# The value products of the decoded streams: probabilities as the stationary operand on four column strips, and one transpose behind

## The chip, the cores and the metric

The kernel runs on one core of a Trainium2 chip. A time is the device time in microseconds (us) of one execution of the whole program; of several executions the median is given. The matrix engine is called PE in the rows, its loading of the stationary operand PEld, VectorE DVE, ScalarE ACT, GpSimd POOL, and the engine that issues most transfers SP.

## What is computed

One step of a hybrid encoder layer: an input projection, three token mixers (banded softmax attention, gated DeltaNet, a diagonal state space model), an output projection and a feed-forward network, for 2048 new prompt frames and for 8 running streams of 16 frames each, all in float32. The change is in the attention of the running streams:

```python
def band_attention_sample(q, k, v, k_cache, v_cache, table):
    kk = jnp.concatenate([k_cache, k], axis=1)      # 512 cached + 16 new rows, 8 heads x 64
    vv = jnp.concatenate([v_cache, v], axis=1)
    s = einsum('bqhd,bkhd->bhqk', q, kk) * d_h ** -0.5 + rel_bias(table, rel)
    p = softmax(s, axis=-1)
    return einsum('bhqk,bkhd->bqhd', p, vv)         # the line that the change is about
```

## The kernel before

The program has three stages in time: the projections together with DeltaNet and the state space model (to about 915 us), the attention (to about 1250 us), and the output projection with the feed-forward network. `attention` goes over 16 tiles of 128 prompt frames (`i`), and in each over 4 pairs of heads (`p`). A round is one pair: scores into PSUM tiles of the pool `asp` (4 buffers, called `aps` in the rows), minimum and exponential (`a_scores`), division by the sum (`a_norm`), transposes of the probabilities through PSUM tiles `tps` (pool `atp`, 3 buffers) into `PT` (`a_turn`), and the products with the values into `aob` (`a_values`). Rounds overlap: the values of a round are written two rounds after its scores.

In the tiles i = 1 to 8 one decoded stream (b = i - 1) is worked beside the prompt: `s_scores` and `s_norm` at p = 0, `s_turn` at p = 1, `s_values` at p = 2. The 8 heads are handled as 4 pairs. The probabilities of a stream stand in one tile `sP` of 128 rows (4 pairs x 2 heads x 16 frames) by 528 keys; `s_turn` transposes them into `sPT` (5 blocks of keys by 128 rows). `sV` holds the cached values (4 blocks of 128 keys by 512 columns, one head each 64 columns), `sVn` the new ones with zero rows below. `s_values` before: for each pair p, five products are summed; the values of the pair (128 keys by 128 columns) are the stationary operand, the 32 columns of the pair in `sPT` move over them, and the result stands with the value columns on the partitions, both heads crossed with both; two copies on VectorE keep the two matching quarters in `sos`, which goes to memory after the eighth stream.

`s_scores` already puts its four pairs on four strips of 32 columns of the array (`ps[p * 32:p * 32 + 32]`), and `a_values` puts its two heads on two strips of 64.

A scheduler sets each engine's order from the program's order and its own estimates, so the rows of an engine can move around an edit, but each engine works its own list in order. The line numbers are those of the kernel before; behind the edit those of the changed kernel are two to six higher.

Of the kernel before, what the change touches and what calls it, by code (L numbers as in the profile page):

```python
# [9 lines left out]
F32 = mybir.dt.float32  # L10
# [31 lines left out]
class K:  # L42
# [1027 lines left out]
    def attention(self, es):  # L1070
        nc, A = self.nc, self.A
        c = self.pool("ac", 1, es=es, side="right")
        self.ak = self.pool("ak", 2, es=es, side="right")
        self.asp = self.pool("asp", 4, PSUM, es=es, side="right")
        self.sc = self.pool("sc", 1, es=es)
        self.sw = self.pool("sw", 1, es=es)
        self.aw = self.pool("aw", 2, es=es)
        self.atp = self.pool("atp", 3, PSUM, es=es)
        self.aop = self.pool("aop", 1, PSUM, es=es)
        nb = self.nb = c.tile([128, 8, 640], F32, name="nb", tag="nb")  # L1080
        r = A["relrev"]
        for h in range(8):
            rv = self.aw.tile([128, 1024], F32, name="rv", tag="qd")[:, 0:640]
            nc.sync.dma_start(rv, bass.AP(tensor=r.tensor, offset=r.offset + h * 767, ap=[[1, 128], [1, 640]]))
            nc.scalar.activation(nb[:, h], rv[:, ::-1], AF.Copy, scale=-1.0)
        nc.gpsimd.memset(nb[0:64, :, 576:640], 1e30)
        nc.gpsimd.memset(nb[64:128, :, 0:64], 1e30)
        self.vt, self.ld_ = {}, {}

        self.kst = [c.tile([128, 8, 512], F32R, name=f"kst{i}") for i in range(2)]  # L1090
        for k in self.kst:
            nc.gpsimd.memset(k[:, :, 128:192].bitcast(F32), 0.0)

        self.qlz = [c.tile([128, 8, 128], F32R, name=f"qlz{i}") for i in range(2)]
        for z in self.qlz:
            for q in range(2):
                nc.gpsimd.memset(z[64 - q * 64:128 - q * 64, q::2].bitcast(F32), 0.0)
        self.sample_setup(es)
        for k in range(2):
            self.a_load_k(k)  # L1100
            self.a_keys(k)
        self.a_load_q(0)
        t = self.a_tile(0)
        for q in range(2):
            self.a_queries(t, q)


        rounds = []
        sample = None
        self.s_load_k(0)  # L1110
        self.s_load_v(0)
        for i in range(16):
            b = i - 1
            streams = 0 <= b < 8
            t1 = None
            for p in range(4):
                if p == 0:
                    if i < 14:
                        self.a_load_k(i + 2)
                    if i < 15:  # L1120
                        self.a_load_q(i + 1)
                elif p == 1 and i < 14:
                    self.a_keys(i + 2)
                elif p == 2 and i < 15:
                    t1 = self.a_tile(i + 1)
                    self.a_queries(t1, 0)
                elif p == 3 and i < 15:
                    self.a_queries(t1, 1)
                if streams and p == 0:
                    sample = self.s_scores(b)  # L1130
                    if b < 7:
                        self.s_load_k(b + 1)
                if streams and p == 2:
                    self.s_values(b, sample)
                    if b < 7:
                        self.s_load_v(b + 1)
                rounds.append(self.a_scores(t, p))
                self.a_norm(rounds[-1])
                if streams and p == 0:
                    self.s_norm(sample)  # L1140
                if len(rounds) > 2:
                    self.a_values(rounds.pop(0))
                if len(rounds) > 1:
                    self.a_turn(rounds[0])
                if streams and p == 1:
                    self.s_turn(sample)
                if p == 3 and i >= 8:
                    self.w_part(i - 8)
            t = t1
            if i == 8:  # L1150
                nc.sync.dma_start(self.mixT[0:512, SEQ:NT].rearrange("(f p) t -> p f t", p=128), self.sos)

        w0 = c.tile([128, 5, 8, 128], F32, name="w0", tag="nb")
        self.a_values(rounds.pop(0))
        self.a_turn(rounds[0])
        self.a_values(rounds.pop(0))
        self.y0 = self.wp.tile([128, 8, 128], F32, name="y0", tag="wor")
        h, l = (w0[:, i].bitcast(F32R) for i in (1, 2))
        self.w_in(0, w0[:, 0], self.y0, h, l)
        self.w_tile(0, self.y0, h, l, lambda: self.asp.tile([128, 512], F32, name="aps", tag="s"))  # L1160
# [177 lines left out]
        nc.gpsimd.memset(PT[:, 4], 0.0)  # L1338
        self.nc.vector.tensor_copy(PT[0:16, 4], ps[0:16, 0:128])

    def s_values(self, b, s):
        PT, vt = s["PT"], self.sV
        ob = self.asp.tile([128, 4, 128], F32, name="aps", tag="s")

        for p in range(4):
            out, hs, qs = ob[:, p, 0:32], slice(p * 128, p * 128 + 128), slice(p * 32, p * 32 + 32)
            for j in range(4):
                self.nc.tensor.matmul(out, vt[:, j, hs], PT[:, j, qs], start=j == 0, stop=False)
            self.nc.tensor.matmul(out, self.sVn[:, hs], PT[:, 4, qs], start=False, stop=True)
        bs = slice(b * 16, b * 16 + 16)  # L1350
        for q in range(2):
            rr = slice(q * 64, q * 64 + 64)
            self.nc.vector.tensor_copy(self.sos[rr, :, bs], ob[rr, :, q * 16:q * 16 + 16])


    def rsqrt1(self, pool, var, eps, tag, pin):
# [542 lines left out]
```

## Time and profile before

| | |
|---|---|
| median of 3 runs | 2916.17 us (2914.97 to 2923.32) |
| the profiled execution | 2905.62 us |
| its span, first to last instruction | 2903.8 us |
| busy: PE, DVE, ACT, POOL | 2787.1, 1946.7, 1314.6, 1096.8 us |
| mean granted clock of PE | 0.983 |

The profile gives, for one execution, when each instruction ran on its engine, what it waited for, and the clock that was granted to the matrix engine as a share of 2.4 GHz (0.50 is 1.2 GHz). A float32 product is recorded as two passes, so a count of PE in a view is twice the number of products in the code; a transpose is one pass. A view by stretches gives, for each stretch, its length, the busy time of each engine in it, the granted clock, and what the transfers did.

### The profile page before, as it was taken

The numbers are of one execution on the slowest core, as the hardware profiler recorded it, in microseconds if no ns is written. First come the engines' busy times: TensorE is split into PE (matmuls) and PEld (weight loads), VectorE is DVE, ScalarE is ACT, GpSimd is POOL, SyncE is SP. The second block draws the span as 40 slices with busy tenths as digits, with TensorE's granted clock in tenths as the row PEclk, the third lists the DMA queues.
The fourth block names the chain that finished last, engine by engine and source line by source line (L and its number), as shares of the span: only waits on it lengthen the run. The fifth ranks groups of instructions, "written<-read, shape, count | busy, mean of one in ns | idle before, by whom it ended". The sixth has DMA issues, their size and how long they took to land.

```text
span 2903.8 us, 46362 instructions
## 1 busy us (share of the span) xinstructions
PE 2787.1 (96%) x16677; PEld 2453.4 (84%) x16677; DVE 1946.7 (67%) x4908; ACT 1314.6 (45%) x2735; POOL 1096.8 (38%) x972
## 2 busy tenths in 40 slices
PE   8999999989989999999999999999999999999998
PEld 8988888867767777888889899889989988888897
DVE  7587887797652677868855555565666566566666
ACT  3554454343354667712243343354434435444443
POOL 0011111241211122102554444456555554777674
PEclk9999999999998899999999999999999999999999
DMA  5634454464556542144542122153322224322321
GB/s 184 202 107 122 111 128 121 136 170 134 157 175 221 158 146 67 45 160 156 189 156 69 58 76 70 59 179 126 102 73 87 88 66 162 144 94 95 115 82 58
DMA packets 292429, 351.89 MB, mean 121 GB/s; under 512 B 85586, under 2 KB 218534, under 8 KB 291878
## 3 DMA queue, kind: packets, MB, share of 16 engines
q1 hardware_dynamic: 292198, 348.92, 38.2%
q8 instruction: 131, 2.15, 0.3%
q14 instruction: 100, 0.82, 0.1%
HBM read 276.58 MB, written 74.89 MB: 121 GB/s over the span
## 4 chain that ended last, share of the span: by engine, by line
PE 69%; DVE 12%; POOL 6%; DMA 6%; issue 4%; ACT 3%; SPq 1%; DVEq 0%; ACTq 0%; POOLq 0%
PE fdp L66 7%; PE fdp L65 7%; PE fdp L67 7%; PE pps L67 3%; PE pps L66 3%; PE pps L65 3%; PE wops L65 2%; PE wops L66 2%; PE wops L67 2%; PE aob L1262 2%; PE fupz L67 2%; PE fupv L65 2%; PE fupv L66 2%; PE tps L1246 2%; PE fupv L67 2%
## 5 line engine op out<-in xcount | busy, mean ns | idle before, releaser
L1542 POOL TENSOR_TENSOR wu<-wur,wu 128x512 fp32r<-128x512 f32 x315 | 424.3, 1351 | 528.0 <-ACT wu L1541 527.0
L1660 DVE TENSOR_TENSOR fy<-fy,fdp 128x512 f32<-128x512 f32 x500 | 342.4, 687 | 271.3 <-PE fdp L67 269.7
L65 PE MATMUL fdp<-wdh,hh 128*128 128x512 f32 x1020 | 398.2, 391 | 1.9 <-DVE fy L1660 1.9
L66 PE MATMUL fdp<-wdl,hh 128*128 128x512 f32 x1020 | 397.6, 390 | 0.0
L67 PE MATMUL fdp<-wdh,hl 128*128 128x512 f32 x1020 | 397.5, 390 | 0.0
L1541 ACT CAST wu<-wur 128x512 fp32r<-128x512 f32 x315 | 194.0, 617 | 445.7 <-DMA wur<-in_w_upL 199.8
L65 PE MATMUL pps<-xh,wh 128*128 128x384 f32 (+2 forms) x800 | 279.9, 352 | 11.6 <-ACT xh L60 9.9
L66 PE MATMUL pps<-xl,wh 128*128 128x384 f32 (+2 forms) x800 | 279.7, 350 | 2.5 <-DVE xl L61 2.3
L67 PE MATMUL pps<-xh,wl 128*128 128x384 f32 (+2 forms) x800 | 278.0, 348 | 0.4 <-DVE wl L61 0.3
L65 PEld LDWEIGHTS fdp<-wdh,hh 128*128 128x128 f32 x1020 | 191.5, 188 | 42.0 <-DVE fy L1660 3.7
L67 PEld LDWEIGHTS fdp<-wdh,hl 128*128 128x128 f32 x1020 | 191.6, 188 | 39.9
L1607 DVE TENSOR_TENSOR hl<-fre,hh 128x384 fp32r<-128x384 f32 (+1 forms) x180 | 161.2, 897 | 93.2 <-ACT hh L1606 92.3
L66 PEld LDWEIGHTS fdp<-wdl,hh 128*128 128x128 f32 x1020 | 191.6, 188 | 37.6
L60 ACT CAST wdh<-wdr 128x1024 fp32r<-128x1024 f32 x94 | 97.9, 1050 | 176.5 <-PE fdp L67 173.4
L65 PEld LDWEIGHTS pps<-xh,wh 128*128 128x128 f32 x800 | 152.0, 191 | 24.5 <-ACT xh L60 11.6
L61 DVE TENSOR_TENSOR wl<-wr,wh 128x512 fp32r<-128x512 f32 (+1 forms) x152 | 108.0, 720 | 87.5 <-ACT wh L60 83.9
L66 PEld LDWEIGHTS pps<-xl,wh 128*128 128x128 f32 x800 | 152.1, 190 | 14.5 <-DVE xl L61 5.7
L67 PEld LDWEIGHTS pps<-xh,wl 128*128 128x128 f32 x800 | 152.1, 190 | 12.0 <-DVE wl L61 2.1
L61 DVE TENSOR_TENSOR wdl<-wdr,wdh 128x1024 fp32r<-128x1024 f32 x94 | 142.4, 1522 | 11.9 <-ACT wdh L60 8.8
L60 ACT CAST wh<-wr 128x512 fp32r<-128x512 f32 (+1 forms) x152 | 92.4, 619 | 78.7 <-DMA wr<-in_w_inA 33.8
L1227 ACT ACTIVATE P<-P,st 128x640 f32<-128x640 f32 (+4 forms) x128 | 97.2, 760 | 63.1 <-DVE st L1224 62.5
L1602 ACT ACTIVATE fre<-fre,ld_b_up 128x384 f32<-128x384 f32 (+1 forms) x144 | 85.9, 597 | 84.9 <-DVE fre L1611 59.5
(556 smaller groups left out, 7390.7 us busy)
## 6 DMA issues: line engine op xcount, KB each, us to landing
wdr<-in_w_dnL SPq DMA_DIRECT2D x96, 512.0 KB
wur<-in_w_upL SPq DMA_DIRECT2D x92, 512.0 KB
wr<-in_w_inA SPq DMA_DIRECT2D x70, 512.0 KB
TU<-tD SPq DMA_DIRECT2D x34, 256.0 KB
y<-in_x SPq DMA_DIRECT2D x17, 512.0 KB
x<-y SPq DMA_DIRECT2D x17, 512.0 KB
fxr<-x SPq DMA_DIRECT2D x17, 512.0 KB
fy<-x SPq DMA_DIRECT2D x17, 512.0 KB
```

What stands on the lines that cost most here:

```text
L60: nc.scalar.copy(hi, src)
L61: nc.vector.tensor_tensor(lo, src, hi.bitcast(F32), OP.subtract)
L65: mm(out, lh, rh, start=first, stop=False, **kw)
L66: mm(out, lh, rl, start=False, stop=False, **kw)
L67: mm(out, ll, rh, start=False, stop=last, **kw)
L1227: self.nc.scalar.activation(x, x, AF.Exp, scale=-1.0, bias=st[:, q:q + 1], accum_out=st[:, 2 + q:3 + q])
L1246: self.nc.tensor.transpose(ps[:, k * 128:(k + 1) * 128], P[:, q, j * 128:(j + 1) * 128], self.ident)
L1541: self.nc.scalar.copy(hi, src)
L1542: P.tensor_tensor(lo, src, hi.bitcast(F32), OP.subtract)
L1602: nc.scalar.activation(r, src, AF.Relu, bias=self.bu[:, c * 2 + i:c * 2 + i + 1])
L1607: V.tensor_tensor(hl, r, hh.bitcast(F32), OP.subtract)
L1660: V.tensor_tensor(y, y, ps[x], OP.add)
```

## The change

`s_values` swaps the operands: the 32 columns of a pair in `sPT` are the stationary operand, the 128 value columns of the pair move, and the result of pair p stands on the partitions 32p to 32p + 31. The loop over the key blocks is now the outer one, so four products in a row go to four different strips. ScalarE copies the 128 x 128 result into the first 128 columns of `sP`. A new step `s_out`, written one round later (p = 3), transposes it on the matrix engine into a `tps` tile, and the two VectorE copies into `sos` read that.

```diff
                 if streams and p == 2:
-                    self.s_values(b, sample)
+                    self.s_values(sample)
                     if b < 7:
                         self.s_load_v(b + 1)
+                if streams and p == 3:
+                    self.s_out(b, sample)
                 rounds.append(self.a_scores(t, p))
...
-    def s_values(self, b, s):
+    def s_values(self, s):
         PT, vt = s["PT"], self.sV
-        ob = self.asp.tile([128, 4, 128], F32, name="aps", tag="s")
-
-        for p in range(4):
-            out, hs, qs = ob[:, p, 0:32], slice(p * 128, p * 128 + 128), slice(p * 32, p * 32 + 32)
-            for j in range(4):
-                self.nc.tensor.matmul(out, vt[:, j, hs], PT[:, j, qs], start=j == 0, stop=False)
-            self.nc.tensor.matmul(out, self.sVn[:, hs], PT[:, 4, qs], start=False, stop=True)
+        ob = s["ob"] = self.asp.tile([128, 512], F32, name="aps", tag="s")
+        for j in range(5):
+            v = vt[:, j] if j < 4 else self.sVn
+            for p in range(4):
+                ps = slice(p * 32, p * 32 + 32)
+                self.nc.tensor.matmul(ob[ps, 0:128], PT[:, j, ps], v[:, p * 128:p * 128 + 128], start=j == 0, stop=j == 4)
+        self.nc.scalar.copy(s["P"][:, 0:128], ob[:, 0:128])
+
+    def s_out(self, b, s):
+
+        ps = self.atp.tile([128, 512], F32, name="tps", tag="t")
+        self.nc.tensor.transpose(ps[:, 0:128], s["P"][:, 0:128], self.ident)
+        src = ps[:, 0:128].rearrange("r (p q s) -> r p q s", q=2, s=16)
         bs = slice(b * 16, b * 16 + 16)
         for q in range(2):
             rr = slice(q * 64, q * 64 + 64)
-            self.nc.vector.tensor_copy(self.sos[rr, :, bs], ob[rr, :, q * 16:q * 16 + 16])
+            self.nc.vector.tensor_copy(self.sos[rr, :, bs], src[rr, :, q])
```

On the matrix engine, first stream, before: a row names the line, what is written, and behind the arrow the moving and then the stationary operand; the pairs one after another, each with its five products.

```order
L1348 MATMUL aps<-sPT,sV 128x32 [waits DMAHW7_49,Activation_49]
L1348 MATMUL aps<-sPT,sV 128x32 x3
L1349 MATMUL aps<-sPT,sVn 128x32 [waits DMAHW0_49,DVE_49]
L1348 MATMUL aps<-sPT,sV 128x32 x4
L1349 MATMUL aps<-sPT,sVn 128x32
```

The last two rows come twice more, and then the prompt's scores. The same place after:

```order
L1352 MATMUL aps<-sV,sPT 32x128 [waits DMAHW7_49,Activation_49]
L1352 MATMUL aps<-sV,sPT 32x128 x15
L1352 MATMUL aps<-sVn,sPT 32x128 [waits DMAHW0_49,DVE_49]
L1352 MATMUL aps<-sVn,sPT 32x128 x3
L1224 MATMUL aps<-kst_11563,qd 128x256
L1225 MATMUL aps<-kst_11563,qlz_11568 128x256
L1224 MATMUL aps<-kst_11563,qd 128x256
L1225 MATMUL aps<-kst_11563,qlz_11568 128x256
L1248 MATMUL tps<-ld_c_ident,P 128x128 [waits PE_49]
L1248 MATMUL tps<-ld_c_ident,P 128x128 x3
L1358 MATMUL tps<-ld_c_ident,sP 128x128 [waits Activation_49]
```

The products are still twenty, with the shapes exchanged, and the new transpose (L1358) stands behind two scores of the prompt and four transposes, waiting for ScalarE.

On ScalarE, fourth stream, before: `woh` are casts of weights for the later output projection.

```order
L1335 COPY sPT<-tps 128x512 [waits PE_49,Activation_49]
L60 CAST woh<-wor 128x512
L1227 ACTIVATE P,st<-P,st 128x640 [waits DVE_49] x2
L1249 COPY PT<-tps 128x512 [waits PE_49,Activation_49,Pool_49]
L1249 COPY PT<-tps 128x256 [waits PE_49]
```

The same place after:

```order
L1337 COPY sPT<-tps 128x512 [waits PE_49,Activation_49]
L60 CAST woh<-wor 128x512 [waits DMAHW4_49]
L60 CAST woh<-wor 128x512
L1353 COPY sP<-aps 128x128 [waits PE_49]
L1229 ACTIVATE P,st<-P,st 128x640 [waits DVE_49] x2
L1251 COPY PT<-tps 128x512 [waits PE_49,Activation_49,Pool_49]
```

The new copy (L1353) stands ahead of the prompt's exponentials, and here behind a cast that waits for a transfer.

## Rows read from the trace of the kernel before

**Rows 1.** The page: busy time of the engines, and granted clock in 40 slices.

```profile
PE 2787.1 (96%) x16677; PEld 2453.4 (84%) x16677; DVE 1946.7 (67%) x4908; ACT 1314.6 (45%) x2735; POOL 1096.8 (38%) x972
PEclk9999999999998899999999999999999999999999
```

**Rows 2.** The chain of waits, 925 to 1135 us: shares by line, and one piece.

```profile
by line: PE aps L1348 17.1%; PE aob L1262 12.2%; PE tps L1246 11.4%; PE aps L1222 8.2%; PE aps L1223 6.7%; DVE P L1236 5.9%; DVE P L1224 5.8%; PE aps L1349 4.4%; issue 4.3%; ACT P L1227 4.2%; PE aps L1316 3.7%; DVE PT L1251 3.2%; ACT PT L12
...
996.37 3.58 DMA wor<-in_w_out
```

**Rows 3.** The eight bursts of s_values: PE, PEld, DVE, ACT, POOL busy; clock, DMA share, GB/s.

```profile
934.29:942.78 8.49, 8.49 (x42) 8.49 (x40) 0.00 (x0) 0.00 (x0) 0.46 (x2) 0.50 0.13 38
955.72:960.18 4.46, 4.46 (x41) 4.46 (x40) 0.00 (x0) 2.14 (x4) 1.29 (x1) 1.00 0.20 43
977.27:982.51 5.24, 5.24 (x41) 5.24 (x41) 0.69 (x1) 2.34 (x4) 1.27 (x1) 0.84 0.17 51
1003.75:1008.24 4.49, 4.49 (x41) 4.49 (x40) 0.69 (x1) 0.22 (x1) 0.00 (x0) 0.99 0.36 117
1032.60:1037.41 4.81, 4.81 (x43) 4.81 (x43) 0.79 (x4) 0.62 (x1) 0.00 (x0) 1.00 0.33 110
1056.32:1062.06 5.74, 5.74 (x41) 5.74 (x42) 0.33 (x1) 1.14 (x2) 0.00 (x0) 0.77 0.21 74
1082.87:1087.92 5.05, 5.05 (x41) 5.05 (x40) 0.00 (x0) 0.00 (x0) 0.00 (x0) 0.88 0.00 2
1111.18:1117.14 5.96, 5.96 (x41) 5.96 (x40) 0.00 (x0) 0.00 (x0) 0.00 (x0) 0.74 0.00 0
sum 44.24, PE 44.24 PEld 44.23 DVE 2.50 ACT 6.46 POOL 3.02; mean PE 5.53 PEld 5.53 DVE 0.31 ACT 0.81 POOL 0.38
```

**Rows 4.** PE in order of time, inside the fifth burst: start, length, what.

```profile
1033.51 0.42 PE L1222 MATMUL aps<-kst,qd 128*128 128x384 f32 x1
1033.77 0.34 PE L1223 MATMUL aps<-kst,qlz 128*128 128x384 f32 x1
1033.95 0.30 PE L1349 MATMUL aps<-sPT,sVn 128*128 128x32 f32 x2
```

**Rows 5.** PE in order of time, four scores of the fourth stream on strips.

```profile
989.33 1.10 PE L1316 MATMUL aps<-sK,sQ 128*32 128x264 f32 x16
990.36 0.50 PE L1222 MATMUL aps<-kst,qd 128*128 128x512 f32 x1
```

**Rows 6.** PE in order of time, values and transposes of one round without a stream.

```profile
1144.21 1.31 PE L1262 MATMUL aob<-PT,vt 128*64 128x128 f32 x20
1145.45 1.31 PE L1246 MATMUL tps<-ld_c_ident,P 128*128 128x128 f32 x10
1146.52 0.37 PE L1222 MATMUL aps<-kst,qd 128*128 128x256 f32 x1
```

**Rows 7.** By stretches, eight stretches right behind the bursts: the fifth, and the sum.

```profile
1037.41:1042.00 4.59, 4.59 (x42) 4.15 (x43) 4.15 (x15) 2.95 (x7) 0.00 (x0) 1.00 0.76 222
...
1117.14:1120.80 3.66, 3.66 (x18) 3.10 (x18) 2.43 (x9) 0.92 (x2) 0.00 (x0) 0.50 0.25 72
sum 33.56, PE 33.56 PEld 28.23 DVE 20.31 ACT 11.99 POOL 0.00; mean PE 4.20 PEld 3.53 DVE 2.54 ACT 1.50 POOL 0.00
```

**Rows 8.** By stretches, from `aob` copy to `aob` copy: tile 5 (stream), 9 (none).

```profile
1029.30:1052.10 22.80, 22.11 (x214) 18.80 (x213) 17.51 (x59) 15.89 (x36) 5.76 (x6) 1.00 0.50 153
...
1133.30:1148.90 15.60, 14.84 (x153) 12.77 (x152) 14.41 (x49) 14.16 (x33) 5.37 (x4) 1.00 0.16 50
```

**Rows 9.** Groups by shape, 926 to 1134 us: busy, mean ns, idle before and releaser.

```profile
L1249 ACT COPY PT<-tps 128x512 f32<-128x512 f32 x32 | 18.3, 573 | 21.3 <-issue 12.2 <-PE tps L1246 8.9
...
L1249 ACT COPY PT<-tps 128x256 f32<-128x256 f32 x20 | 7.3, 366 | 0.1
...
L1353 DVE COPY sos<-aps 64x64 f32<-64x64 f32 x16 | 3.5, 222 | 42.0 <-PE aps L1349 41.9
```

**Rows 10.** Waits of PE, 925.9 to 1133.3 us: total, times, longest.

```profile
PE aob L1262 <- ACT PT L1249: 2.6, 4, 1.1
```

## The prediction

> **What bounds the kernel now.** I read the page first: the matrix engine is busy for 96% of the span, VectorE for 67%, ScalarE for 45% [rows 1]. The granted clock is 9 or more tenths in all slices but two neighbours, and those two lie where the attention begins (871 to 1016 us), with the decoded streams in it. The second view is the chain of waits over the tiles with streams: the two lines of s_values, L1348 and L1349, hold 21.5% of it, more than any other line [rows 2]. So these products are on the path that sets the end, not beside it. The third view is that of the stretches, one for each of the eight bursts of s_values [rows 3]: the matrix engine is busy in all of each burst, VectorE in 2.50 of 44.24 us and ScalarE in 6.46. Nothing runs long enough beside a burst to take its place if it shrinks.
>
> What a burst is made of can be read from the second stretch, at full clock: 40 passes in 4.46 us, 0.11 us each. A pass moves only 32 columns, but it loads 128 columns of values first, and PEld is busy for the whole stretch [rows 3]: the loads set the pace. The bursts at lower clock are longer, up to 8.49 us where the clock is 0.50 (1.2 GHz).
>
> **What the change removes.** The 44.24 us of the bursts, less two scores of the prompt that ran inside the fifth: from 1033.51 to 1033.95 us, 0.44 us [rows 4]. That is 43.80 us of matrix engine time.
>
> **What it adds on the matrix engine.** Again 40 passes per stream, with 32 columns loaded and 128 moved, four neighbours on four strips. The trace of before has no such form, but two near ones. The prompt's values are 20 passes that move the same 128 columns, two neighbours on two strips of 64: they take 1.24 us to the start of what follows, against 1.07 us for 10 transposes, which move 128 columns on the full width one after the other [rows 6]. Twenty passes in the time of ten: the pairs run side by side. The scores of a stream are 16 passes of 264 columns on four strips in 1.03 us [rows 5]; one after another at the pace of a transpose (0.107 us for 128 columns) they would be 16 x 0.22 = 3.5 us. So four strips run side by side too. For the new burst both rows give the same: ten groups of four in place of ten groups of two, 1.24 us; or 1.03 x 128/264 x 40/16 = 1.25 us. The bounds are 1.07 us (ten groups with no entry or exit) and 40 x 0.107 = 4.3 us (no two side by side). I take 1.24, the nearest row. The new transpose is one pass of 0.11 us [rows 6]. Per stream 1.35 us, for eight 10.8 us at full clock; at half clock throughout it would be 21.6.
>
> **First term: 43.8 - 10.8 = 33.0 us saved**, with 22.2 as its lower end by the clock.
>
> The twenty passes of the values cost 0.17 us more than ten times the pace of a transpose (1.24 - 1.07): what entering and leaving the strips takes there [rows 6]. The Trainium skill, "TensorEngine Tiling (Array Packing)", Key Properties, says that a change of the tiling mode drains the engine, and this change adds one: strips of 64, then of 32, then full width, where before it was 64 and then full width. The trace agrees in direction with its 0.17 us. By the row the price is inside the 1.24 us; by the rule one more switch per stream would be 8 x 0.17 = 1.4 us, an estimate, and the saving of the first term 31.6.
>
> **Second term, the clock behind the bursts.** I took the eight stretches right behind the bursts, up to where the clock rises again. In seven of them it stands at 0.50 to 0.53, as in the last; only behind the fifth it is 1.00 [rows 7]. The engine is busy in all of these 33.56 us. Without the fifth they are 28.97 us at about half clock, which at full clock would be 14.5 us less. What the engine did before the clock fell was a burst of s_values, 128 loaded for 32 moved. No row shows what a strip burst of 1.24 us leaves behind it. The ends are 0 and 14.5; I take half, 7 us, since I have no row that is nearer to one end.
>
> **Third term, what is now waited for.** The result leaves by a longer way: ScalarE copies it, the matrix engine transposes it, VectorE copies it out. The VectorE copies keep their size (0.22 us, 16 of them). The ScalarE copy has 128 x 128; the line through 573 ns for 512 columns and 366 for 256 [rows 9] gives some 0.26 us, an estimate, eight times 2.1 us on an engine that has room. In each engine's order after the change, the transpose stands behind two or more scores of the prompt and at least four of its transposes, over a microsecond of work at the pace of rows 6. The copy needs its 0.26 us and some hand-over, so it is ready by then, if ScalarE is free. If not, the matrix engine stands at the transpose, with the prompt's scores, and so VectorE's minima and ScalarE's exponentials, queued behind. One more place waits: the fourth score tile behind a burst needs the PSUM buffer that the ScalarE copy frees; before, a VectorE copy freed it. Where the matrix engine now waits for a ScalarE copy, it does so for 2.6 us in 4 waits, the longest 1.1 [rows 10]. Eight streams with one such wait of the mean length, 0.65 us, are 5 us; the ends are 0 and 8 x 1.1 = 8.8. A late transfer of weights is the one larger stall that I find: the chain holds 3.58 us of waiting for `wor` [rows 2], and in the fourth stream the copy now stands behind a cast that waits for such a transfer. That can go or come back, 3.6 us either way. I take 5 us in all.
>
> **Whether another engine takes over.** Tile 5 has a stream and full clock: 22.8 us, PE 22.11, VectorE 17.51. Tile 9 has no stream: 15.6 us with PE 14.84 and VectorE 14.41, 92% of it [rows 8]. At that share tile 5 could fall to 17.51 / 0.92 = 19.0 us, a room of 3.8, while the first term takes 4.81 - 0.44 - 1.35 = 3.0 from it. So VectorE comes close but doesn't bind. Behind the attention the engine is busy for over 90% of nearly every slice of the page, so time won here isn't lost there to a later wait. Transfers: the share is 0.50 in tile 5 [rows 8], and would be some 0.58 in a tile of 19.8 us.
>
> **The sum.** 33.0 + 7 - 5 = 35 us. The profiled execution took 2905.6 us, which gives 2870.6. It lies 10.6 us under the median of the runs (2916.2); what differs is not in the profile, so I carry the saving to the median: 2881 us.
>
> **Rivals.**
>
> The clock stays down: the burst and what follows it run at half clock as now. Then the first term is 22.2, the second 0, less 5: 17 us, **2899**. For it: seven of eight stretches behind the bursts are at half clock [rows 7], the first burst is at 0.50 from its start, and the strips leave VectorE's waits as they are. Against it: tile 9, the same work without a burst, has 1.00 throughout [rows 8]. Chance 0.16.
>
> The strips don't run side by side, so the change doesn't do what it says: 40 x 0.107 + 0.11 = 4.4 us per stream, 35.1 for eight, saves 8.7, less 5: 4 us, **2912**. Against it are two lines that do run side by side [rows 5, 6]. Chance 0.06.
>
> The way out becomes the bound, and it gets slower: ScalarE works in order, and if its copy stands each time behind an exponential or a cast that isn't ready, the matrix engine stands at the transpose. The point from which this decides is 33.0 / 8 = 4.1 us per stream. With 5 us each the loss is 40 against 33, **2923**. For it: one wait of 3.58 us for a transfer [rows 2]. The Trainium skill, "TensorEngine Tiling (Array Packing)", PSUM Bottleneck, warns that tiling speeds up the matrix engine but not the emptying of PSUM, which may become the bound; here the chain of the streams is shortened at 3 us per tile only. Against it: ScalarE is idle for 21.3 us before its copies of `PT` in these tiles, and more than half of that isn't for want of the matrix engine [rows 9]; in four of eight streams the copy stands directly behind the copy of `sPT`, which s_values waits for anyway. Chance 0.05.
>
> **How the numbers follow.** The forecast, 2881, has 0.73. Its best end is 33.0 + 14.5 + 3.6 = 51 us, 2865. Its worst is 22.2 - 8.8 - 3.6 = 10 us, 2906, but that takes every bad end at once; the range reaches past the rival of the clock, to 2901. The serial and the slower rival (0.11) and the far ends stay out. A measurement of this kernel tells 0.3%, some 9 us, from no change: faster below 2907.4. Forecast and clock rival are faster, 0.89; the serial one is no change, 0.06; the last is slower, 0.05.
>
> **What would show it.** In the profile after, a burst of L1352 takes 1.2 to 1.4 us at clock 1.00, with starts in fours; above 4 us the strips are serial and the first term is wrong. The stretches behind the bursts at 1.00 show the second term at its upper end, at 0.50 at its lower. PE waiting for ACT `sP` at L1358 for over 1 us each shows the third term too small. Tile 5 should shrink from 22.8 to about 20 us, and tile 9 should keep its 15.6. If tile 5 shrinks and the end doesn't come earlier by the sum of the tiles, the gain was lost behind the attention, and the argument from the page was wrong.

## The result

| kernel | median, us | kernel before on the same chip, us | ratio (95% interval) | first score to last copy of `aob` in the profile, us |
|---|---|---|---|---|
| changed | 2864.16 | 2916.17 | 0.9838 (0.9819 to 0.9856) | 285.6 |
| changed, a second chip | 2863.62 | 2906.25 | 0.9854 (0.9837 to 0.9872) | 287.1 |
| before | | | | 331.4 |

The change makes the kernel 1.5 to 1.6% faster. It gains 52 us by the first pair of medians, 42.6 us by the second, and 42.7 us between the two profiled spans (2903.8 and 2861.1). The medians of the changed kernel agree within 0.6 us. Those of the kernel before differ by 10 us between the chips, and nothing in a profile explains that; I work with 43 to 46 us, which the traces account for. The predicted 2881 was too slow, and the first median is 0.8 us below the range.

The page of the changed kernel, against [rows 1]: the clock has no slice under 9 tenths any more.

```profile
PE 2739.1 (96%) x16685; PEld 2404.6 (84%) x16685; DVE 1945.7 (68%) x4908; ACT 1316.4 (46%) x2743; POOL 1096.7 (38%) x972
...
PEclk9999999999999999999999999999999999999999
```

The first view to read is that by stretches, once for the whole attention: before, and then after (length, busy PE, PEld, DVE, ACT, POOL, clock, DMA share, GB/s).

```profile
915.20:1246.60 331.40, 304.92 (x2620) 253.14 (x2619) 238.61 (x785) 218.08 (x498) 67.30 (x71) 0.91 0.35 107
```

```profile
915.40:1201.00 285.60, 258.81 (x2628) 205.36 (x2627) 234.47 (x785) 219.51 (x506) 67.96 (x71) 0.98 0.41 125
```

The attention is 45.8 us shorter. The matrix engine's busy time fell by 46.1 us, its idle time went from 26.5 to 26.8. So all of the gain is busy time of the matrix engine, and none of it was given back to waits. Behind the attention the output projection and the feed-forward network together took some 3 us more in this execution, hence 42.7 in the span.

The bursts of s_values after, against [rows 3]; three of the eight, and their sum.

```profile
933.91:935.14 1.23, 1.23 (x42) 1.03 (x40) 0.00 (x0) 0.00 (x0) 0.46 (x2) 1.00 1.14 340
946.58:947.81 1.23, 1.23 (x41) 1.03 (x40) 0.00 (x0) 0.91 (x2) 0.86 (x1) 1.00 0.66 148
...
1070.93:1072.16 1.23, 1.23 (x41) 1.03 (x41) 0.00 (x0) 0.00 (x0) 0.00 (x0) 1.00 0.00 0
sum 9.84, PE 9.84 PEld 8.25 DVE 2.15 ACT 1.81 POOL 1.32; mean PE 1.23 PEld 1.03 DVE 0.27 ACT 0.23 POOL 0.17
```

All eight take 1.23 us, all at clock 1.00. From the end of the first low stretch to the end of the attention the clock is never lower again, as the stretch of the changed kernel shows:

```profile
930.50:1201.00 270.50, 247.81 (x2562) 198.55 (x2563) 225.83 (x744) 208.85 (x474) 62.58 (x63) 1.00 0.40 119
```

The gain then splits so. Bursts: 43.80 - 9.84, less eight transposes of 0.11, is 33.1 us. The other 13.0 of the 46.1 us are what remains: the same work as before, now at full clock, so what the clock took outside the bursts. Nearly all of that lies behind them; one low stretch of before stands behind a wait of 1.83 us for VectorE (`sst`) instead, and holds at most 1.7 us of it:

```profile
1021.83:1025.24 3.41, 3.41 (x26) 2.86 (x26) 2.44 (x11) 2.79 (x6) 1.27 (x1) 0.50 1.01 382
```

The 33.1 hold clock too. Eight old bursts at full clock are 8 x 4.46 = 35.7 us, so 8.1 of the 43.80 were the clock. Of the 46.1 us, about 25 are the shorter bursts and 21 the clock.

### The profile page after: what moved, and what is told of

Read it like the earlier page. It is cut to its first block, busy times and chain, and to the rows that moved or that the text cites. A ratio compares the mean times of both kernels' runs of the same rounds, so it can differ in the third digit from the quotient of the medians.

```text
span 2861.1 us, 46393 instructions
## 1 busy us (share of the span) xinstructions
PE 2739.1 (96%) x16685; PEld 2404.6 (84%) x16685; DVE 1945.7 (68%) x4908; ACT 1316.4 (46%) x2743; POOL 1096.7 (38%) x972
## 4 chain that ended last, share of the span: by engine, by line
PE 70%; DVE 12%; POOL 5%; DMA 5%; ACT 4%; issue 4%; SPq 1%; DVEq 0%; ACTq 0%; POOLq 0%
PE fdp L66 7%; PE fdp L65 7%; PE fdp L67 7%; PE pps L66 3%; PE pps L67 3%; PE pps L65 3%; PE wops L66 2%; PE wops L65 2%; PE wops L67 2%; PE fupv L65 2%; PE fupv L66 2%; PE fupv L67 2%; PE fupz L67 2%; PE bqs L649 2%; PE fupz L66 2%
```

## Experiments

What was open after this: whether the 33 us come from the strips running side by side or from the shorter loads; what made the clock fall, the length of a burst or what its passes move; whether the longer way out costs anything; and whether VectorE is now the bound. All profiles cited are of the kernel named ahead of them.

| kernel | median, us | before, same chip, us | ratio (interval) | attention, us | PE busy in it, us |
|---|---|---|---|---|---|
| before | | | | 331.4 | 304.9 |
| changed | 2863.62 | 2906.25 | 0.9854 (0.9837 to 0.9872) | 285.6 | 258.8 |
| loops exchanged | 2880.41 | 2906.32 | 0.9917 (0.9902 to 0.9932) | 302.4 | 273.3 |
| full width | 2892.52 | 2906.32 | 0.9952 (0.9937 to 0.9967) | 315.1 | 285.9 |
| old, in halves | 2889.09 | 2906.32 | 0.9939 (0.9923 to 0.9955) | 311.3 | 285.3 |
| old, 64 moved | 2892.37 | 2903.59 | 0.9953 (0.9936 to 0.9971) | 317.2 | 288.7 |
| strips, four times | 2896.31 | 2906.25 | 0.9968 (0.9954 to 0.9982) | 319.7 | 287.9 |
| straight out | 2862.02 | 2906.32 | 0.9851 (0.9835 to 0.9868) | 284.7 | 257.4 |
| out at once | 2870.14 | 2906.25 | 0.9877 (0.9858 to 0.9895) | 290.1 | 260.4 |
| weights on GpSimd | 2868.70 | 2906.25 | 0.9871 (0.9853 to 0.9889) | 291.7 | 263.8 |

The last two columns come from one profile each (that of the changed kernel is the first). Kernels of different chips are compared by their ratios.

One thing touches every comparison of profiles with the changed kernel. In all six kernels made from it by an edit, the matrix engine waits once, ahead of the eighth burst, for 2.1 to 2.4 us for VectorE's `sst`; in the two profiles of the changed kernel no such wait is longer than 0.65 us. In five of the six (not in loops exchanged) the clock then stands at 0.50 for 3.4 us, which costs 1.7 us at most. Why the changed kernel is spared it no run shows; since edits so different share it, 2 to 4 us of attention above the changed kernel say little about any one of them. The waits for `sst` (total, times, longest) in the kernel before, the changed one, straight out and out at once, and the low stretch of straight out:

```profile
PE aps L1222 <- DVE sst L1317: 3.5, 4, 1.8
PE aps L1224 <- DVE sst L1319: 1.5, 3, 0.6
PE aps L1223 <- DVE sst L1318: 2.8, 2, 2.2
PE aps L1223 <- DVE sst L1318: 3.1, 3, 2.2
1058.72:1062.14 3.42, 3.42 (x27) 3.02 (x26) 1.95 (x10) 2.21 (x6) 0.34 (x1) 0.50 0.26 77
```

### The changed kernel again

> The changed kernel again, for a comparison on the same chip with the three kernels sent with it. Theory (gain = first term 33 plus the whole of the clock, 13): in its profile the eight bursts take 1.23 us each at clock 1.00 and 44 to 46 us fewer lie before the feed-forward network; ratio to the kernel before 0.983 to 0.986. Rival (part of the 52 us between the first medians was the runs, not the kernel): ratio nearer to 0.985 than to 0.982; only the spread tells.

It gave 0.9854, with the intervals of the two measurements overlapping from 0.9837 to 0.9856. Its attention takes 287.1 us; the difference to 285.6 lies in the first tile with a stream: the low stretch is as long as in the first profile (10.2 us), but it came later and covers more of that tile, which took 20.3 us against 18.3. The gain is nearer to 43 than to 52 us.

### Loops exchanged: one strip at a time

```diff
-        for j in range(5):
-            v = vt[:, j] if j < 4 else self.sVn
-            for p in range(4):
-                ps = slice(p * 32, p * 32 + 32)
+        for p in range(4):
+            ps = slice(p * 32, p * 32 + 32)
+            for j in range(5):
+                v = vt[:, j] if j < 4 else self.sVn
```

> The changed kernel with the two loops of s_values exchanged: pair outside, key block inside, so ten passes in a row go to the same strip of 32 columns. Same products, same loads, same result. Theory (the first term is the strips running side by side): passes on one strip run one after another, 40 x 0.107 = 4.3 us per burst instead of 1.23, eight times 3.05 = 24 us above the changed kernel's 2864 if the granted clock stays at 1.00, about 2888. Rival 1 (the gain of the burst comes from the shorter loads, 32 columns instead of 128): burst about 1.2 us, 2864. Rival 2 (a long burst that uses a part of the array makes the clock fall): burst 4.3 us and more, stretches behind the bursts at 0.50, another 12 to 14 us, about 2901.

The second burst by stretches:

```profile
949.20:952.47 3.27, 3.27 (x42) 3.07 (x41) 0.00 (x0) 0.91 (x2) 1.29 (x1) 1.00 0.40 98
```

3.27 us and not 1.23, with the same loads, the same columns moved and the same clock: rival 1 falls, the shorter loads alone don't make the burst as short as that. Nor is it the 4.3 us of the theory. The matrix engine in order of time shows why:

```profile
949.21 1.09 PE L1352 MATMUL aps<-sV,sPT 128*32 128x128 f32 x10
950.10 0.27 PE L1352 MATMUL aps<-sVn,sPT 128*32 128x128 f32 x1
950.13 0.27 PE L1352 MATMUL aps<-sV,sPT 128*32 128x128 f32 x1
950.21 0.27 PE L1352 MATMUL aps<-sVn,sPT 128*32 128x128 f32 x1
```

The new rows of a pair (`sVn`) are its last two passes, and passes of the next pair (`sV`) already start before and between them. The engine starts the next strip's passes early where two strips meet, but inside a strip they stand in line. The price against the changed kernel: 302.4 - 285.6 = 16.8 us of attention, against 8 x 2.04 = 16.3 from the bursts. The clock stayed at 1.00 behind the bursts, so rival 2 falls too. About half of the 33 us remains with the loops this way round; their order is worth the other half. What remains is 43.80 - 8 x 3.27 = 17.6 us before the transposes: 8.1 for the clock that no longer falls in the bursts, and 9.5 for 3.27 against 4.46, which is the overlap where strips meet.

### Full width

```diff
         for j in range(5):
             v = vt[:, j] if j < 4 else self.sVn
-            for p in range(4):
-                ps = slice(p * 32, p * 32 + 32)
-                self.nc.tensor.matmul(ob[ps, 0:128], PT[:, j, ps], v[:, p * 128:p * 128 + 128], start=j == 0, stop=j == 4)
-        self.nc.scalar.copy(s["P"][:, 0:128], ob[:, 0:128])
+            self.nc.tensor.matmul(ob, PT[:, j], v, start=j == 0, stop=j == 4)
+        for p in range(4):
+            ps = slice(p * 32, p * 32 + 32)
+            self.nc.scalar.copy(s["P"][ps, 0:128], ob[ps, p * 128:p * 128 + 128])
```

> The swap of the operands without strips: all 128 columns of a key block of sPT are loaded at once and all 512 value columns move, 5 products of 512 columns; the four matching quarters are copied out of PSUM by four ScalarE copies of 32 rows. Three quarters of the products are thrown away. Theory: ten passes of 4 x 0.107 us are 4.3 us per burst, 24 us above the changed kernel, and eight times three more copies on ScalarE beside; the clock stays at 1.00, since the array is worked over its full width: about 2888. Rival (any burst of 4 us makes the clock fall behind it): another 12 to 14 us, about 2901.

```profile
970.50:974.47 3.97, 3.97 (x10) 1.82 (x11) 0.59 (x1) 0.11 (x1) 0.00 (x0) 1.00 0.39 134
974.47:979.00 4.53, 4.53 (x33) 2.93 (x31) 3.89 (x11) 4.34 (x12) 0.00 (x0) 1.00 0.77 243
```

The burst and the stretch right behind it, here the third: 3.97 us, and the clock at 1.00 in both. A burst of 4 us by itself doesn't bring the clock down. The attention is 29.5 us longer than the changed one, of which the bursts are 8 x 2.74 = 21.9. The other 7.6 us I haven't split; three more ScalarE copies per stream, the wait of 2.43 us for `sst` and the low stretch of the clock behind it, ahead of the eighth burst, are in it.

### The old products in two halves

```diff
                 if streams and p == 2:
-                    self.s_values(b, sample)
+                    self.s_values(b, sample, 0)
+                if streams and p == 3:
+                    self.s_values(b, sample, 2)
                     if b < 7:
                         self.s_load_v(b + 1)
...
-        for p in range(4):
+        for p in range(p0, p0 + 2):
```

> The kernel before with its s_values cut in two: pairs 0 and 1 at p = 2, pairs 2 and 3 one round later (p = 3), so the same products of 32 moved columns come in bursts of 2.2 us with scores and transposes of the prompt between. Theory (the second term, some 13 us, is the clock that falls when a whole burst of 4.5 us moves few columns): the half-clock stretches become fewer or vanish, at best 8 + 13 = 21 us under the kernel before, 2895; the first term (33 us less 8 for the bursts at low clock) stays away. Rival (the clock falls for the number of such passes, however they are cut): same as before, 2916 within 6 us.

The matrix engine in order of time, at the third stream, with the prompt's scores and transposes between the halves:

```profile
978.14 0.39 PE L1351 MATMUL aps<-sPT,sVn 128*128 128x32 f32 x2
978.36 0.47 PE L1224 MATMUL aps<-kst,qd 128*128 128x512 f32 x1
...
979.38 1.04 PE L1248 MATMUL tps<-ld_c_ident,P 128*128 128x128 f32 x8
980.25 0.98 PE L1350 MATMUL aps<-sPT,sV 128*128 128x32 f32 x8
```

and the stretch with the second to the eighth stream:

```profile
960.00:1118.00 158.00, 146.60 (x1357) 121.84 (x1356) 122.77 (x393) 106.78 (x235) 38.41 (x40) 1.00 0.45 143
```

The clock is 1.00 over all of it. Only in the first stream did it fall: the first half began at 936.89 and ran at 1.00, and right behind it the clock went down, for the second half and what followed.

```profile
939.50:949.70 10.20, 10.20 (x54) 8.24 (x55) 2.85 (x15) 3.60 (x11) 1.29 (x1) 0.50 0.34 112
```

So the same forty passes per stream, cut by 2 us of other work, no longer bring it down in seven of eight streams. That is worth 20.1 us of attention and 17 us of the median (2906.32 to 2889.09), against 21 at best. So the clock's share is real, and it can be had without touching the products.

### The old products with 64 columns moved

```diff
-            out, hs, qs = ob[:, p, 0:32], slice(p * 128, p * 128 + 128), slice(p * 32, p * 32 + 32)
+            out, hs, qs = ob[:, p, 0:64], slice(p * 128, p * 128 + 128), slice(p // 2 * 64, p // 2 * 64 + 64)
```

> The kernel before with 64 columns moved in each pass of s_values instead of 32: the two pairs that lie side by side in sPT move over the values of one pair, and half of the result is thrown away (four small VectorE copies instead of two take the rest). Same number of passes, same wide loads, same place. Theory 1 (the loads set the pace, 0.11 us per pass, and the clock falls since the passes move few columns): bursts of 4.46 us at full clock, and with twice the columns the clock stays at 1.00 more often; at best 8 + 13 = 21 us less than before, less 2 us for the copies: about 2887, like the halves. Theory 2 (the clock falls for the form of the passes, a wide load before each short move, whatever they move): the bursts and what is behind them at 0.50 as before, 2906 to 2910.

The first two bursts, the stretch behind the second, and all from there to the end of the streams:

```profile
939.76:948.25 8.49, 8.49 (x42) 8.49 (x40) 0.00 (x0) 0.00 (x0) 0.16 (x1) 0.50 0.19 71
961.58:966.04 4.46, 4.46 (x41) 4.46 (x41) 0.69 (x1) 2.65 (x5) 2.13 (x3) 1.00 0.29 88
966.04:970.00 3.96, 3.96 (x32) 2.68 (x31) 3.20 (x15) 2.40 (x8) 0.00 (x0) 1.00 0.75 223
...
960.00:1123.80 163.80, 150.58 (x1377) 123.39 (x1376) 121.58 (x394) 109.16 (x239) 38.80 (x43) 1.00 0.43 136
```

Seven of eight bursts take 4.46 us, to the hundredth what the old burst takes at full clock, so moving twice the columns costs no time at all: the wide loads set the pace, as the prediction read it. And the clock stays at 1.00 in and behind all seven. With 32 columns, seven bursts began at 1.00 too, and the clock fell in or right behind six of them [rows 3, rows 7]. Nothing else about the passes differs. Theory 2 falls. That this is no accident of one profile, the mean granted clock of every run says: 0.989 to 0.991 in the four runs of this kernel, 0.981 to 0.984 in the seven of the kernel before on the same chip. The first burst began while the clock was low already, and ran at 0.50 to its end. To the halves the kernel lacks 5.9 us (317.2 against 311.3). Its low stretches are 3.4 us longer in all, which is 1.7 us of that at most; the rest I haven't split.

### The strips four times over

```diff
-        for j in range(5):
-            v = vt[:, j] if j < 4 else self.sVn
-            for p in range(4):
+        for r in range(4):
+            for j in range(5):
+                v = vt[:, j] if j < 4 else self.sVn
+                for p in range(4):
```

> The changed kernel with the twenty products of every burst done four times over (each time from the start, so the result is the same). The burst becomes as long as that of the kernel before at full clock, but on four strips with 128 moved columns. Theory (the clock fell for what the burst did, few moved columns behind wide loads, and not for its length alone): burst 40 groups of 0.109 = 4.4 to 4.5 us at clock 1.00, none of the stretches behind at 0.50; eight times 3.27 = 26 us above the changed kernel of the same call, minus what the engines beside use of it (0 to 4). Rival (any burst of 4.5 us of products with few columns, loaded or moved, makes the clock fall): bursts and what is behind at 0.50 as before, 26 + 13 = 39 us or more above.

The second burst, the stretch behind it, and the fourth burst:

```profile
947.22:951.73 4.51, 4.51 (x162) 4.31 (x161) 1.29 (x2) 2.05 (x4) 1.31 (x1) 1.00 0.58 162
951.73:956.00 4.27, 4.16 (x35) 2.79 (x31) 2.09 (x7) 1.96 (x6) 0.00 (x0) 1.00 0.79 254
994.18:999.23 5.05, 5.05 (x161) 4.77 (x161) 1.29 (x2) 1.14 (x2) 0.00 (x0) 0.88 0.28 97
```

A burst of strips as long as the old one leaves the clock at 1.00 behind it. Seven of the eight bursts began at 1.00, and in or behind none of them did the clock fall; the one at 994.18 began in a low stretch that had started before it. The time is 32.7 us above the changed kernel, where 22 to 26 were expected and 39 would have been the rival's, so the time alone doesn't decide between them; the clock does. Against the changed kernel's profile of the same chip (287.1 us, busy 259.3) the attention is 32.6 us longer: 28.6 us are busy time of the matrix engine, of which two low stretches of 3.4 us hold at most 3.4, and 4.0 are idle, of which one wait for `sst` holds 2.1.

### Straight out

This kernel leaves out the ScalarE copy and the transpose, and takes `s_out` right behind the burst, so the results of the streams land untransposed; only its time is of use.

```diff
-        self.nc.scalar.copy(s["P"][:, 0:128], ob[:, 0:128])
...
-        ps = self.atp.tile([128, 512], F32, name="tps", tag="t")
-        self.nc.tensor.transpose(ps[:, 0:128], s["P"][:, 0:128], self.ident)
-        src = ps[:, 0:128].rearrange("r (p q s) -> r p q s", q=2, s=16)
+        src = s["ob"][:, 0:128].rearrange("r (p q s) -> r p q s", q=2, s=16)
```

> The changed kernel without the longer way out: no ScalarE copy and no transpose, VectorE copies quarters of the untransposed result straight from PSUM into sos right behind s_values (what lands there is a part of the right numbers in the wrong places). Theory (the third term was put too high: in the trace after nothing waits for the ScalarE copy): at most 8 x 0.11 = 1 us of transposes and a PSUM buffer in the rotation, 0 to 3 us under the changed kernel's 2864. Rival (the way out costs the 5 us of the prediction, hidden as waits for VectorE and for tps buffers): 2859 or less.

0.9851 against 0.9854: no difference that the runs can tell. In the profiles the attention is 0.9 us shorter, as much as eight transposes take; the idle time of the matrix engine is 27.3 us against 26.8. But this profile holds the wait of 2.2 us for `sst` and the low stretch, which the changed kernel's doesn't. So the medians show no cost of the way out, and the profiles leave room for some 4 us. That the cost is small is seen directly on ScalarE in the trace of the changed kernel, behind the burst that ends at 1049.78:

```profile
1049.92 0.27 ACT L1353 COPY sP<-aps 128x128 f32<-128x128 f32 x1 [2.03 <-PE aps L1352]
1051.89 0.83 ACT L1229 ACTIVATE P<-P,st 128x640 f32<-128x640 f32 x1 [1.71 <-DVE st L1226]
```

ScalarE stands ready for 2 us, copies in 0.27 us, 0.14 us after the burst, and then has to wait for VectorE anyway. The transpose that needs the copy starts 3 us later:

```profile
1053.34 0.33 PE L1358 MATMUL tps<-ld_c_ident,sP 128*128 128x128 f32 x1 [0.30 <-ACT PT L1251]
```

Its wait is for a `tps` buffer that the prompt's copy still holds, 0.30 us, not for `sP`. Over all eight streams this transpose waits three times, 1.2 us in all, each time for that:

```profile
PE tps L1358 <- ACT PT L1251: 1.2, 3, 0.4
```

### Out at once

```diff
                 if streams and p == 2:
                     self.s_values(sample)
+                    self.s_out(b, sample)
...
-                if streams and p == 3:
-                    self.s_out(b, sample)
```

> The changed kernel with the transpose written directly behind the burst (p = 2) and not one round later; on the matrix engine one and a half or two score tiles of the prompt then stand between them in most streams. Theory (the ScalarE copy is done 0.4 us behind the burst in the trace after, so the wait is short wherever the transpose stands): 0 to 2 us above the changed kernel of the same call. Rival (the copy is late and the later place hides it, the third term's mechanism): 8 x 0.65 = 5 us above or more, with the matrix engine waiting for ScalarE's sP at the transpose.

6.5 us slower by the medians, but with intervals that overlap (0.9858 to 0.9895 against 0.9837 to 0.9872), and 1.2 us by the spans of the profiles. The wait that the rival names is small, as the source view of the transpose shows (idle time before it, times):

```profile
  ACT sP L1352: 0.9, 5
```

So the direct wait is 0.9 us in all. Against the changed kernel on the same chip the attention is longer by 3.0 us and the idle time of the matrix engine by 1.9; the wait for `sst` and the low stretch behind it are as much as that. Whether the place of the transpose costs anything stays open. It is no reason to move it.

### Weights on GpSimd: is VectorE the next bound?

```diff
-            self.split(self.woh[:, k, ns], self.wol[:, k, ns], wr[:, ns])
+            nc.scalar.copy(self.woh[:, k, ns], wr[:, ns])
+            nc.gpsimd.tensor_tensor(self.wol[:, k, ns], wr[:, ns], self.woh[:, k, ns].bitcast(F32), OP.subtract)
```

> The changed kernel with the low halves of the output projection's weights (wol, 16 subtractions of 128 x 512 in the tiles 4 to 15, 0.68 us each on VectorE) computed on GpSimd, which is mostly idle there. Nothing is left out. Theory 1 (VectorE comes close but does not bind, as the prediction said): within 2 us of the changed kernel of the same call. Theory 2 (with the bursts gone the tiles with a stream are held by VectorE: the matrix engine waits for its row sums and copies 9 + 3 times, 7.5 us in all, in the trace after): 3 to 8 us faster than the changed kernel. Rival to both: the subtractions take 1.3 us and more on GpSimd and are late for nothing, but slow VectorE down while both run: 2 to 5 us slower.

Not faster: 0.9871 against 0.9854, 5 us slower by the medians, with intervals that overlap. The group of VectorE's row scaling, 960 to 1088 us, in the changed kernel and then in this one:

```profile
L1238 DVE TENSOR_SCALAR P<-P,rs 128x640 f32<-128x640 f32 x42 | 24.0, 611 | 0.1
```

```profile
L1238 DVE TENSOR_SCALAR P<-P,rs 128x640 f32<-128x640 f32 x38 | 25.0, 700 | 0.2
```

The means hide two kinds. Most scalings take 0.55 us in both kernels; 4 of the 42 and 6 of the 38 take 0.8 to 1.7 us, and each of these has a subtraction of GpSimd beside it (not every scaling beside one is slow). Only two of the six stand beside a moved subtraction; the others meet the prompt's `qlz` and `kst`, which GpSimd computes in both kernels. The two, on VectorE, and what GpSimd did then:

```profile
1025.78 3.07 DVE L1238 TENSOR_SCALAR P<-P,rs 128x640 f32<-128x640 f32 x2
1025.62 2.74 POOL L1430 TENSOR_TENSOR wol<-wor,woh 128x512 fp32r<-128x512 f32 x2 [2.56 <-issue]
```

VectorE lost 16 instructions of 0.68 us, 10.9 us, but its busy time in the attention fell only from 234.5 to 229.8. The clock also fell in three places behind its first low stretch in this execution, and the wait for `sst` is there. Theory 2, that VectorE holds the tiles with a stream, finds no support, but the test took too little from VectorE to refute it. The changed kernel remains the best of those measured that compute everything.

## Why the prediction was right, and where it was off

The bound and the mechanism held. s_values was on the path: its 43.80 us of bursts and transposes became 10.7, and the attention got shorter by that and more. Point by point:

- **First term, 33.0 us.** Measured 33.1. The burst took 1.23 us where 1.24 was taken from the two rows of other strips; loops exchanged shows that half of the term hangs on neighbours going to different strips, and 64 moved columns that the loads paced the old form. The worry for the lower end, strips at half clock, didn't come about, except that in the second execution the first burst took 1.57 us.
- **Second term, 7 us.** This is the step that failed in size: it was 13.0 us. I had the ends 0 and 14.5 and took the middle for want of a nearer row. There was one that I passed over: the fifth burst ran as long as the others at clock 1.00, but with two score products inside it, 0.44 us [rows 4], and alone of the eight had no fall behind it [rows 7]. The halves fit it: old passes cut by other work left the clock at 1.00 in seven of eight streams. That row spoke for the upper end.
- **Third term, 5 us of new waits.** Also off: the idle time of the matrix engine grew by 0.3 us, and straight out is no faster by its runs. The new transposes wait for 1.2 us in all; the waits for `sst` fell from 3.5 to 1.5 us at the same time, and why they fell no run shows. The mean wait for ScalarE [rows 10] was that of other copies; before the new copy ScalarE stood idle in all eight streams, for 11.0 us in all. The rows said so: beside five of the eight bursts ScalarE was busy for 0.62 us or less [rows 3].
- **The sum.** 33.1 + 13.0 - 0.3 = 45.8 us in the attention, against 35. Both errors went the same way.
- **Other engines.** VectorE comes close, and no run shows it to bind: in the changed kernel it is busy for 234.5 of 285.6 us, the matrix engine waits no longer than before, and taking a little work from VectorE didn't help. Tile 5 did not shrink to 20 us between its copies of `aob`, but from 22.8 to 22.4; what held it was not followed. Tile 9 took 15.8 us against 15.6. The tiles 1 to 8 together went from 207.4 to 162.3 us, so single tiles were the wrong place to check.
- **The rivals.** Clock that stays down: refuted, 1.00 in all eight bursts and behind them. Serial strips: refuted. The way out as the bound, with the warning of the Trainium skill ("TensorEngine Tiling (Array Packing)", PSUM Bottleneck) behind it: no sign of it; with 45.1 us less in the eight tiles the copy is still done before its transpose could start, as the 0.30 us above show. The switch of the tiling mode that the Trainium skill ("TensorEngine Tiling (Array Packing)", Key Properties) names costs no more than the 1.24 us already held: the burst took 1.23 with entry and exit.
- **The carry to the median.** The saving of the profile matches the second pair of medians to 0.1 us. Against the first pair it is 9 us short, for the 10 us by which the kernel before was slower there; that stays open.

## What to carry to other kernels

Where short moves stand behind wide loads, swap the operands, put the products on strips, and let neighbours in the program go to different strips: the same forty passes took 4.46 us, 3.27 us with the loops the wrong way round, and 1.23 us. When the granted clock falls behind a burst, price the work after it as well as the burst; here the work outside the bursts had 13 of the 46 us and the clock in the bursts 8, and cutting the burst in two, without any other change, gained 20 us by itself. A longer way out of PSUM costs little while the engine that copies is waiting for something else anyway: look at what the copying engine does beside the burst, not at its mean waits.

## What the runs showed of the hardware

- Passes that load 128 columns take 0.11 us whether they move 32 or 64. With 32 the granted clock fell from 1.00 to 0.50 in or right behind six of the seven bursts that began at 1.00, with 64 in or behind none of seven; with 32 and a cut of 2 us in the middle it fell in one of eight streams.
- The clock also fell without such a burst: a stretch of 3.4 us at 0.50 began within 1.2 us behind a wait of the matrix engine of 1.83 us in the kernel before, and of 2.1 to 2.4 us in five others. Behind two such waits (2.17 us in loops exchanged, 2.31 us in the halves) it did not.
- Strips side by side are not only for neighbours in the program: with the pairs one after another, the engine started passes of the next strip before the last ones of the strip before, and a burst took 3.27 us where forty in line would take 4.3.
- VectorE's 128 x 640 scalings take 0.55 us, but 0.8 to 1.7 us in ten cases of the two kernels, each with a subtraction of GpSimd beside it: two in a row beside two of `wol`'s took 3.07 us. GpSimd's subtractions of 128 x 512 took 1.28 us each there, against 0.68 on VectorE.
